# The attention weights of a trunk layer, transposed by DMA in pieces of 1024 keys

## The chip, the core and the metric

The kernel runs on one core of a Trainium2 chip. A core has five engines that work in parallel, each through its own list of instructions in a fixed order: TensorE (PE in the profile, with its weight loads as PEld), VectorE (DVE), ScalarE (ACT), GpSimd (POOL) and SyncE (SP), which here only issues DMA transfers. An instruction that has to wait holds up everything behind it on its engine. The metric is the device time of one execution in microseconds (us), lower is better, and times of several runs are given as their median.

## The reference, cut to what matters

One layer of a hybrid encoder: an RMSNorm and one input projection feed three mixers (a diagonal state-space layer S5, a differential attention, a gated linear recurrence HGRN2). Their outputs are joined, projected, and added to the stream; a gated MLP with a short convolution follows. The sequence has 2048 tokens of width 1024; the attention has 6 heads, the MLP 2816 hidden channels. The change lies in the attention:

```python
def attend(args):
    q_blk, blk = args
    q_pos = blk * Q_BLOCK + jnp.arange(Q_BLOCK)                     # Q_BLOCK = 128
    sc = jnp.einsum('bqhcd,bkhcd->bhcqk', q_blk, k).astype(jnp.float32) * scale
    dist = jnp.abs(q_pos[:, None] - k_pos[None, :]).astype(jnp.float32)
    visible = (k_pos[None, :] // CHUNK) <= (q_pos[:, None] // CHUNK)
    bias = jnp.where(visible[None], -slopes[:, None, None] * dist[None], MASK_VALUE)
    p = jax.nn.softmax(sc + bias[None, :, None], axis=-1)
    w = p[:, :, 0] - lam * p[:, :, 1]
    return jnp.einsum('bhqk,bkhd->bqhd', w, v)
```

Each head has two softmax maps; their difference `w` weighs the values. To multiply `w` by `v`, TensorE needs `w` with the keys on the partitions, but it comes out with the queries there: `w` has to be transposed.

## The kernel before, in words

**The attention.** `phase_attn` (L754) is called twice: a first pass for the query blocks i = 0 to 7, whose rows have L = 128 (i + 1), so up to 1024 keys, and a second pass for i = 8 to 15 with 1152 to 2048 keys. Each pass goes over 6 heads and 8 query blocks, so 48 units of one head and one block. In the second pass there are four score buffers (`t_sc`, two a unit) and two buffers for transposed weights (`t_wt`). A unit is worked in these steps:

- *Scores* (L816): TensorE makes 512 scores at a time (`t_ps`, L832). VectorE adds the bias, writes them to `t_sc`, and keeps a running maximum `t_mx` (L836), each chunk waiting for the one ahead of it. ScalarE takes the exponential of the whole row (L848), once for each of the two maps.
- *Joined* (L854): VectorE forms the difference of the two maps in float32, 1024 keys at a time (L867).
- *Parts* (L881): the float32 weights are split into two float16 parts. For each piece of at most 1024 keys ScalarE casts the high part (L890) and GpSimd subtracts it from the weights, which gives the low part (L891). Both lie in the memory of the second map's scores, the low part LM = 128 · 16 = 2048 elements behind the high part. Behind the loop over pieces SP issues two DMA transposes (L898), one for the high part and one for the low part of the whole row, both from `t_sc` to `t_wt`. A transposed block is 128 x 128.
- *Values* (L904): TensorE multiplies the transposed blocks by the values (`t_po`, L913), in chunks of four blocks: eight products with the high part first, then four with the low part. ScalarE copies the result out (L875, L877).

**What runs beside it.** `weave` (L2084) puts the steps of the attention among those of the other phases: the recurrence (`g_` tiles), the output projection (`o_`), and the MLP (`f_`). The MLP's up and gate projections are the `f_pm` matmuls of L96; its weights are brought through DRAM tiles `Wd` by SP (L143 stores, L148 loads). The down-projection is the `f_pd` matmuls of L1786; in its first half its weights are streamed, `f_dst` loads by SP (L1713), cast to `f_dw`, and its activations come as `f_da` (L1757). The last units of the second pass run beside this half.

**What sets the order.** The program is not run in the order in which it is written. The framework's scheduler fixes a list of instructions for each engine by its own estimate of when each can start. A change to one phase can thus move instructions of all phases on all engines. A transpose on SP waits there until its source is written (by ScalarE, or by GpSimd for the low part); behind it wait the loads and stores of all phases.

Of the kernel before, what the change touches and what calls it, by code (L numbers as in the profile page):

```python
# [753 lines left out]
def phase_attn(K, A, QKd, Vd, Yd, i0, i1, s_bufs, lean):  # L754
# [5 lines left out]
    tc, nc = K.tc, K.nc  # L760
    V = nc.vector
    NT = i1 - i0
    LM = 128 * i1
    base, nlam, lk, gc = A.base, A.nlam, A.lk, A.gc
    with ExitStack() as es:
# [9 lines left out]
        def stack(a, i, parts, h, cols):  # L775
            for r, e in enumerate(parts):
                nc.sync.dma_start(
                    out=a[32 * r:32 * r + 32],
                    in_=QKd[i, e, h * HD:(h + 1) * HD, cols].rearrange("(c r) t -> r c t", c=2),
                )  # L780
# [73 lines left out]
        def joined(h, i, sc):  # L854

            H = heads[h]
            n_ = i - i0
            L = 128 * (i + 1)
            a = mp.tile([128, 2], F32, tag="a", name="t_a")
            V.reciprocal(out=a[:, 0:1], in_=H.la[:, 1, n_:n_ + 1])  # L860
            V.tensor_scalar(
                out=a[:, 1:2], in0=H.la[:, 0, n_:n_ + 1], scalar1=a[:, 0:1], scalar2=nlam[:, 0:1],
                op0=ALU.mult, op1=ALU.mult,
            )
            for k0 in range(0, L, 1024):
                k1 = min(L, k0 + 1024)
                V.scalar_tensor_tensor(  # L867
                    out=sc[0][:, k0:k1], in0=sc[1][:, k0:k1], scalar=a[:, 1:2],
                    in1=sc[0][:, k0:k1], op0=ALU.mult, op1=ALU.add,
                )  # L870
# [10 lines left out]
        def parts(h, i, sc):  # L881

            joined(h, i, sc)
            yield 1
            L = 128 * (i + 1)
            hl = sc[1].bitcast(F16)
            wt = wp.tile([128, 2, i1, 128], F16, tag="w", name="t_wt")
            for k0 in range(0, L, 1024):
                k1 = min(L, k0 + 1024)
                nc.scalar.copy(hl[:, k0:k1], sc[0][:, k0:k1])  # L890
                nc.gpsimd.tensor_tensor(  # L891
                    out=hl[:, LM + k0:LM + k1], in0=sc[0][:, k0:k1], in1=hl[:, k0:k1],
                    op=ALU.subtract,
                )
                if k1 < L:
                    yield 1
            for w in range(2):
                nc.sync.dma_start_transpose(  # L898
                    out=wt[:, w, 0:i + 1, :], in_=hl[:, LM * w:LM * w + L]
                )  # L900
            sc.append(wt)
            yield 1

        def values(h, i, sc):  # L904
# [4 lines left out]
            for c in range(nb):  # L909
# [9 lines left out]
                yield 1  # L919

        stages = ((parts, 3), (values, 4))

        def norm(h):
# [1211 lines left out]
```

## Time and profile before

| | |
|---|---|
| median of 3 runs | 2716.79 us (2714.36 to 2717.66) |
| profiled execution | 2723.9 us |
| its span | 2722.1 us, mean granted TensorE clock 0.934 |
| second pass of the attention (first to last transpose issued) | 811.8 to 1900.0 us |
| transposes | 192: 96 of 1 to 8 blocks, 96 of 9 to 16 |

The profiled execution took 7.1 us more than the median, and its span is 1.8 us shorter than its own time. The profile counts an engine busy while it executes; the rest of the span it waits, and for each wait the trace names what ended it. In a row of the timeline, the numbers are start and duration in us, then engine, line, operation, output and inputs, shapes and count; in brackets is the idle time of the engine ahead of it and who ended it. "SPq" is SP's issue of a DMA; its duration is the time for which SP was taken up by it, and its landing is the end of the transfer.

### The profile page before, as it was taken

The page shows a single profiled execution, that of the slowest core. Times are in us where ns is not written, and L with a number is a line of the kernel's source. Part 1 is how long each engine was busy: PE and PEld are TensorE (multiplying, and loading weights), DVE is VectorE, ACT ScalarE, POOL GpSimd, SP SyncE. Part 2 cuts the span into 40 slices and gives each one's busy share as a digit, 9 for nine tenths or more (in the row PEclk, how much of TensorE's full clock was granted, in tenths as well). Part 3 has the DMA queues.
Part 4 walks back from the last instruction along what each step waited for, and adds up shares of the span by engine and source line. Part 5 has one row for each costly group of instructions (what it writes and reads, how often), then busy time and mean ns, then how long its engine had stood idle before and what let it go on. Part 6 is the DMA issues. An engine that isn't in the chain of part 4 may idle for free.

```text
span 2722.1 us, 42584 instructions
## 1 busy us (share of the span) xinstructions
PE 2408.0 (88%) x15438; PEld 1354.2 (50%) x15438; DVE 1873.5 (69%) x3401; ACT 1316.9 (48%) x2470; POOL 1350.7 (50%) x1149
## 2 busy tenths in 40 slices
PE   5998898888888889769988898598979999999998
PEld 4655556766766764334443444243434444444444
DVE  7467756688869885597788998865455655545565
ACT  6333344667757663564466766633235433333321
POOL 5688612455444542367677677515313344444280
PEclk8899898888989989879999999699989999999999
DMA  7676555467456666655466665688784655554733
GB/s 240 230 214 207 167 161 126 94 133 143 104 125 137 132 135 177 161 122 182 150 182 169 183 173 170 207 276 256 266 312 148 204 168 154 155 148 136 286 99 123
DMA packets 556740, 473.07 MB, mean 174 GB/s; under 512 B 277297, under 2 KB 433265, under 8 KB 555505
## 3 DMA queue, kind: packets, MB, share of 16 engines
q1 hardware_dynamic: 534352, 429.97, 56.0%
q10 hardware_dynamic: 22176, 40.38, 4.0%
q8 instruction: 121, 1.98, 0.3%
q14 instruction: 91, 0.74, 0.1%
HBM read 290.35 MB, written 125.83 MB: 153 GB/s over the span
## 4 chain that ended last, share of the span: by engine, by line
PE 22%; DVE 15%; issue 8%; POOL 7%; ACT 7%; DMA 6%; SPq 1%; ACTq 0%; DVEq 0%; POOLq 0%
PE f_pd L1786 10%; PE f_pm L96 7%; POOL f_k L1863 2%; DVE f_a L61 2%; DMA f_dst<-in_w_down_dram 2%; DVE t_sc L836 2%; DVE f_t L1617 2%; PE o_pm L1493 2%; PE o_pe L1411 2%; DVE t_sc L867 1%; DVE f_w L63 1%; POOL f_u L1863 1%; ACT f_t L1615 1%; ACT f_t L1910 1%; ACT t_sc L848 1%
## 5 line engine op out<-in xcount | busy, mean ns | idle before, releaser
L96 PE MATMUL f_pm<-f_q,f_w 128*128 128x512 f16 x3696 | 836.8, 386 | 30.0 <-DVE f_u L1863 9.2
L96 PEld LDWEIGHTS <-f_w 128*128 128x128 f16 x3696 | 363.3, 99 | 487.5 <-issue 70.1
L1786 PE MATMUL f_pd<-f_dw,f_da 128*128 128x512 f16 x1848 | 407.1, 382 | 2.7 <-DVE f_r L1764 1.5
L891 POOL TENSOR_TENSOR t_sc<-t_sc 128x1024 f16<-128x1024 f32 (+7 forms) x144 | 250.6, 1753 | 302.3 <-ACT t_sc L890 279.1
L1786 PEld LDWEIGHTS <-f_da 128*128 128x128 f16 x1848 | 181.1, 98 | 226.2 <-issue 14.5
L832 PE MATMUL t_ps<-t_k,t_q 96*128 96x512 f16 (+2 forms) x480 | 165.9, 372 | 94.6 <-DVE t_mx L836 80.2
L848 ACT ACTIVATE t_sc<-t_sc,t_nm 128x128 f32<-128x128 f32 (+7 forms) x192 | 230.5, 1201 | 6.6 <-DVE f_a L61 1.1
L836 DVE CUSTOM_DVE_ANT_0 t_sc<-t_ps,t_base,t_mx 128x512 f32<-128x512 f32 (+3 forms) x288 | 185.2, 643 | 18.9 <-PE t_ps L832 10.8
L61 DVE TENSOR_TENSOR f_a<-f_t,f_a 128x512 f16<-128x512 f32 x132 | 154.8, 1192 | 48.3 <-ACT f_a L55 47.8
L913 PEld LDWEIGHTS <-t_wt 128*128 128x128 f16 x2448 | 106.3, 101 | 121.3 <-DMA t_wt<-t_sc 50.4
L867 DVE SCALAR_TENSOR_TENSOR t_sc<-t_sc,t_a 128x1024 f32<-128x1024 f32 (+7 forms) x144 | 164.6, 1169 | 1.6
L96 PE MATMUL g_pq<-g_h,g_w 128*128 128x256 f16 x1152 | 159.2, 299 | 5.1 <-DVE g_sg L1160 2.7
L1863 POOL TENSOR_TENSOR f_t<-f_t,f_t 128x512 f32<-128x512 f32 x66 | 101.6, 1553 | 123.1 <-ACT f_a L55 108.8
L913 PE MATMUL t_po<-t_v,t_wt 128*128 128x64 f16 x2448 | 120.5, 198 | 47.2 <-DMA t_wt<-t_sc 42.4
L96 PE MATMUL g_pv<-g_w,g_h 128*128 128x256 f16 x1152 | 150.3, 288 | 9.2 <-ACT g_w L55 9.2
L1863 POOL TENSOR_TENSOR f_k<-f_k,f_k 128x512 f32<-128x512 f32 x88 | 124.5, 1414 | 51.5 <-ACT f_halo L1907 25.4
L1617 DVE SCALAR_TENSOR_TENSOR f_t<-f_u,f_cw,f_t 128x1024 f32<-128x1024 f32 x88 | 124.1, 1410 | 33.1 <-ACT f_t L1615 32.3
L836 DVE CUSTOM_DVE_ANT_0 t_sc<-t_ps,t_base 128x512 f32<-128x512 f32 (+2 forms) x192 | 120.4, 631 | 34.4 <-PE t_ps L832 13.7
L890 ACT CAST t_sc<-t_sc 128x1024 f16<-128x1024 f32 (+7 forms) x144 | 111.4, 792 | 64.4 <-DVE t_sc L867 63.4
L55 ACT ACTIVATE f_w<-f_sum 128x512 f16<-128x512 f32 x110 | 69.2, 629 | 146.4 <-DVE f_sum L139 62.2
L96 PEld LDWEIGHTS <-g_w 128*128 128x128 f16 x1152 | 121.3, 107 | 36.2 <-issue 6.4
L96 PEld LDWEIGHTS <-g_h 128*128 128x128 f16 x1152 | 116.8, 103 | 36.8 <-issue 10.8
(335 smaller groups left out, 4475.4 us busy)
## 6 DMA issues: line engine op xcount, KB each, us to landing
f_w<-Wd SPq DMA_DIRECT2D x231, 256.0 KB, 3.0
Wd<-f_w SPq DMA_DIRECT2D x154, 256.0 KB, 2.1
Ad<-f_a ACTq DMA_DIRECT2D x154, 256.0 KB, 2.7
f_da<-Ad SPq DMA_DIRECT2D x42, 768.0 KB, 4.9
g_h<-Hd SPq DMA_DIRECT2D x24, 1024.0 KB, 6.7
f_dst<-in_w_down_dram SPq DMA_DIRECT2D x48, 512.0 KB, 4.9
o_wst<-in_w_out_dram SPq DMA_DIRECT2D x24, 512.0 KB, 5.8
f_wst<-in_w_gate_dram SPq DMA_DIRECT2D x22, 512.0 KB, 5.6
```

The costliest lines, as they stand in the source:

```text
L61: nc.vector.tensor_tensor(out=lo, in0=src, in1=hi, op=ALU.subtract)
L96: nc.tensor.matmul(out=out, lhsT=lhs(a, k), rhs=rhs(b, k), start=(n == 0), stop=(n == 3 * nk - 1))
L832: nc.tensor.matmul(out=ps[:, 0:k1 - k0], lhsT=qt[:, c, 128 * (i % 4):128 * (i % 4) + 128], rhs=H.k[:, c, k0:k1], start=True, stop=True,)
L836: V.tensor_tensor_reduce(out=sc[c][:, k0:k1], in0=ps[:, 0:k1 - k0], in1=bs[:, k0:k1], scale=1.0, scalar=-3e38 if j == 0 else mx[:, c, j - ...
L848: nc.scalar.activation(out=sc[c][:, 0:L], in_=sc[c][:, 0:L], func=AF.Exp, scale=SLOPES[h], bias=nm[:, c:c + 1], accum_out=H.la[:, c, n_:n_ ...
L867: V.scalar_tensor_tensor(out=sc[0][:, k0:k1], in0=sc[1][:, k0:k1], scalar=a[:, 1:2], in1=sc[0][:, k0:k1], op0=ALU.mult, op1=ALU.add,)
L890: nc.scalar.copy(hl[:, k0:k1], sc[0][:, k0:k1])
L891: nc.gpsimd.tensor_tensor(out=hl[:, LM + k0:LM + k1], in0=sc[0][:, k0:k1], in1=hl[:, k0:k1], op=ALU.subtract,)
L913: nc.tensor.matmul(out=po, lhsT=wt[:, w, b, :], rhs=vt[:, b, 64 * v:64 * v + 64], start=(b == 0 and w + v == 0), stop=(b == i and w == 1),)
L1617: V.scalar_tensor_tensor(out=t0, in0=u[:, c:n + c], scalar=cw[:, c, m:m + 1], in1=t0, op0=ALU.mult, op1=ALU.add,)
L1786: nc.tensor.matmul(out=ps[t], lhsT=a[:, q, x, tk], rhs=w[:, y, q, :], start=(first and q + x + y == 0), stop=(last and q == n - 1 and y == 1),
L1863: eng.tensor_tensor(out=o, in0=a, in1=b, op=op)
```

## The change: each piece is transposed as soon as it is split

The two transposes move from behind the loop into it. Each piece of at most 1024 keys gets two transposes of its own, one for the high and one for the low part, right behind the two instructions that split it. In the first pass a row is one piece, so it keeps its two transposes and its order. In the second pass a row of L keys is two pieces, of 1024 and of L − 1024 keys: four transposes a unit instead of two, 192 instead of 96, half of them of 8 blocks and half of 1 to 8. The same blocks are moved, and PE, VectorE, ScalarE and GpSimd have the same instructions as before. In the new kernel the transposes are at line 896.

```diff
             for k0 in range(0, L, 1024):
                 k1 = min(L, k0 + 1024)
                 nc.scalar.copy(hl[:, k0:k1], sc[0][:, k0:k1])
                 nc.gpsimd.tensor_tensor(
                     out=hl[:, LM + k0:LM + k1], in0=sc[0][:, k0:k1], in1=hl[:, k0:k1],
                     op=ALU.subtract,
                 )
+                for w in range(2):
+                    nc.sync.dma_start_transpose(
+                        out=wt[:, w, k0 // 128:k1 // 128, :], in_=hl[:, LM * w + k0:LM * w + k1]
+                    )
                 if k1 < L:
                     yield 1
-            for w in range(2):
-                nc.sync.dma_start_transpose(
-                    out=wt[:, w, 0:i + 1, :], in_=hl[:, LM * w:LM * w + L]
-                )
             sc.append(wt)
             yield 1
```

The scheduler makes a new order with it. Three places on SP, in its list of DMA issues (the last group of numbers is the shape; a transpose of 9 blocks is 128x9x128):

At the start of the second pass (query blocks 8 to 9 of head 0), before:

```order
L898 DMA_TRANSPOSE t_wt<-t_sc 128x9x128
L1386 DMA o_wst<-in_w_out_dram 128x2x512
L898 DMA_TRANSPOSE t_wt<-t_sc 128x9x128
L1106 DMA g_h<-Hd 128x16x256
L898 DMA_TRANSPOSE t_wt<-t_sc 128x10x128
L1358 DMA Yd<-g_yo 256x1x512
```

and now:

```order
L896 DMA_TRANSPOSE t_wt<-t_sc 128x8x128
L896 DMA_TRANSPOSE t_wt<-t_sc 128x1x128
L896 DMA_TRANSPOSE t_wt<-t_sc 128x8x128
L896 DMA_TRANSPOSE t_wt<-t_sc 128x1x128
L1386 DMA o_wst<-in_w_out_dram 128x2x512
L1106 DMA g_h<-Hd 128x16x256
L896 DMA_TRANSPOSE t_wt<-t_sc 128x8x128
L896 DMA_TRANSPOSE t_wt<-t_sc 128x2x128
L1358 DMA Yd<-g_yo 256x1x512
```

The four transposes of the first unit now stand together; the loads that stood between and behind its two stand behind all four.

At the start of the streamed half of the down-projection (head 5, query blocks 11 to 13; `f_dst` are the streamed weights), before:

```order
L898 DMA_TRANSPOSE t_wt<-t_sc 128x12x128
L1713 DMA f_dst<-in_w_down_dram 128x2x512
L1713 DMA f_dst<-in_w_down_dram 128x512
L1713 DMA f_dst<-in_w_down_dram 128x2x512
L1713 DMA f_dst<-in_w_down_dram 128x512
L1757 DMA f_da<-Ad_73 128x3072
L1757 DMA f_da<-Ad_73 128x2048
L898 DMA_TRANSPOSE t_wt<-t_sc 128x12x128
L1713 DMA f_dst<-in_w_down_dram 128x2x512
L1713 DMA f_dst<-in_w_down_dram 128x512
L1713 DMA f_dst<-in_w_down_dram 128x2x512 x2
L898 DMA_TRANSPOSE t_wt<-t_sc 128x13x128
```

and now, from the same load of `f_da` on:

```order
L1757 DMA f_da<-Ad_73 128x3072
L1757 DMA f_da<-Ad_73 128x2048
L896 DMA_TRANSPOSE t_wt<-t_sc 128x8x128
L1713 DMA f_dst<-in_w_down_dram 128x2x512
L896 DMA_TRANSPOSE t_wt<-t_sc 128x5x128
L1713 DMA f_dst<-in_w_down_dram 128x512
L896 DMA_TRANSPOSE t_wt<-t_sc 128x8x128
L1713 DMA f_dst<-in_w_down_dram 128x2x512 x2
L896 DMA_TRANSPOSE t_wt<-t_sc 128x5x128
```

All four transposes of query block 11 (12 blocks) now stand ahead of the first `f_dst` loads, where before its last one stood behind four of them. The eight of query blocks 12 and 13 stand one by one among the loads; those of block 13 (14 blocks) stood further on before.

At the last unit, before:

```order
L1713 DMA f_dst<-in_w_down_dram 128x2x512
L1713 DMA f_dst<-in_w_down_dram 128x512 x3
L898 DMA_TRANSPOSE t_wt<-t_sc 128x16x128
L1757 DMA f_da<-Ad_77 128x3072
L898 DMA_TRANSPOSE t_wt<-t_sc 128x16x128
L1757 DMA f_da<-Ad_77 128x2048
```

and now:

```order
L1713 DMA f_dst<-in_w_down_dram 128x2x512
L1713 DMA f_dst<-in_w_down_dram 128x512 x2
L896 DMA_TRANSPOSE t_wt<-t_sc 128x8x128 x2
L1757 DMA f_da<-Ad_77 128x3072
L1713 DMA f_dst<-in_w_down_dram 128x512
L896 DMA_TRANSPOSE t_wt<-t_sc 128x8x128 x2
L1757 DMA f_da<-Ad_77 128x2048
```

One of the four loads of streamed weights now stands behind the first two transposes.

On TensorE the rows are too many to show; counted, they read so. Of the 48 units of the second pass, 22 have fewer matmuls than before between their last score matmul and their first value matmul, 20 have as many, 6 have more. In heads 0 to 2 (24 units) the number falls by 184 in all. For the last unit the list had eight `t_po`, 22 `f_pd`, and the other 40 `t_po`; now nine `f_pd` stand between the two groups. Two units of the second pass move far: the scores of head 3, query block 10, now stand ahead of a stretch of some 500 matmuls of the up-projection, and the last scores of head 5, query block 13, some 270 matmuls sooner. From about 1910 us of the profiled execution before, behind the attention, the lists hold the same work in nearly the same order.

## The prediction

> **What bounds the kernel now.** First the page's totals and the shares of the chain that ended last, then the stretches in which the second pass of the attention runs.
>
> ```profile
> PE 2408.0 (88%) x15438; PEld 1354.2 (50%) x15438; DVE 1873.5 (69%) x3401; ACT 1316.9 (48%) x2470; POOL 1350.7 (50%) x1149
> PE 22%; DVE 15%; issue 8%; POOL 7%; ACT 7%; DMA 6%; SPq 1%; ACTq 0%; DVEq 0%; POOLq 0%
> ```
>
> PE is busy for 88% of the span, so time is won only where it stands idle. By stretch (start:end, length, then busy time and instructions of PE, PEld, DVE, ACT and POOL, granted clock, DMA share, GB/s):
>
> ```profile
> 806.00:1006.00 200.00, 176.69 (x1919) 137.13 (x1918) 175.00 (x426) 132.49 (x242) 95.23 (x77) 0.92 0.59 125
> 1006.00:1240.00 234.00, 182.46 (x1218) 95.94 (x1219) 162.28 (x321) 125.53 (x237) 103.02 (x68) 0.85 0.64 157
> 1706.00:1760.00 54.00, 27.30 (x164) 12.06 (x164) 46.58 (x90) 33.72 (x58) 27.81 (x19) 0.66 0.64 201
> 1760.00:1910.00 150.00, 136.56 (x788) 63.99 (x787) 86.24 (x129) 54.39 (x84) 50.20 (x25) 0.94 0.86 270
> 1910.00:2722.00 812.00, 778.74 (x3596) 353.80 (x3594) 445.76 (x533) 268.03 (x431) 320.31 (x211) 0.98 0.56 182
> ```
>
> The second pass runs from 806 to 1910. PE idles 23 us in the first of these rows, 52 in the second, 27 in the short one before the streamed down-projection, 13 in the next. Behind 1910 nothing of the change is left. Who ends PE's idle time between 806 and 1910 (total us, times, longest), and from 806 to 1240 alone (last row):
>
> ```profile
> PE t_ps L832 <- DVE t_mx L836: 76.3, 54, 7.3
> PE t_po L913 <- DMA t_wt<-t_sc: 28.5, 14, 6.6
> ...
> PE t_po L913 <- DMA t_wt<-t_sc: 20.2, 11, 4.6
> ```
>
> The largest wait, scores behind the running maximum on DVE, isn't touched. The transposed weights are waited for 28.5 us in 14 places. That is the most that the change can take out of PE's idle time directly; 20.2 us of it lies in heads 0 to 2, before 1240.
>
> **What one transpose costs.** The trace has both sizes: the first pass's transposes move 1 to 8 blocks, the sizes of the new ones (first two rows); the second pass's 9 to 16 (last two). Issue time on SP is min/median/max in ns, landing in us.
>
> ```profile
> L898 SPq DMA_TRANSPOSE t_wt<-t_sc x96: 1120/1218/4422, 435.4 to 765.1; - x96
> DMA to landing us min/median/max: 2.2/3.1/7.7
> ...
> L898 SPq DMA_TRANSPOSE t_wt<-t_sc x96: 1244/1538/6122, 811.8 to 1900.0; - x96
> DMA to landing us min/median/max: 3.2/4.2/11.1
> ```
>
> The last transpose of a unit thus lands 4.2 − 3.1 = 1.1 us sooner after its issue. It also no longer follows one that had to wait for the whole row. What is split ahead of it:
>
> ```profile
> L891 POOL TENSOR_TENSOR t_sc<-t_sc 128x1024 f16<-128x1024 f32 x54 | 126.9, 2354 | 196.4 <-ACT t_sc L890 188.3 <-DVE t_mx L836 5.8 <-DVE rs_t L84 2.3
> L890 ACT CAST t_sc<-t_sc 128x1024 f16<-128x1024 f32 x54 | 56.1, 1042 | 44.8 <-DVE t_sc L867 44.5
> ```
>
> A first high piece need not wait for a second cast (up to 1.04 us) nor a first low piece for a second subtraction (up to 2.35). So the first four-block chunk of values can have its high part 1.1 + 1.04 = 2.1 us earlier, its low part 1.1 + 2.35 = 3.5 us. The last chunk gains 1.1 at most. One wait shows it whole (timeline; bracketed, the wait before it):
>
> ```profile
> 1180.35 9.48 SPq L898 DMA_TRANSPOSE t_wt<-t_sc  x2
> 1185.38 2.87 POOL L891 TENSOR_TENSOR t_sc<-t_sc 128x896 f16<-128x896 f32 x1
> 1187.42 0.40 PE L913 MATMUL t_po<-t_v,t_wt 128*128 128x64 f16 x8
> 1192.46 0.45 PE L913 MATMUL t_po<-t_v,t_wt 128*128 128x64 f16 x5 [4.65 <-DMA t_wt<-t_sc]
> ```
>
> PE does the high products of a chunk at 1187.4 and then stands 4.65 us for the low ones, whose transpose couldn't start before POOL's second piece ended at 1188.25. With pieces the low blocks of that chunk have left when POOL turns to the second piece at 1185.38; landing 1.2 + 3.1 us later they are there by 1189.7, and about 2.8 us of the 4.65 go.
>
> **What of it stays.** The order was made anew by the same planner, and it spends the earlier arrival: of the 48 units of this pass 22 have fewer PE matmuls than before between their last score and their first value matmul, 20 as many, 6 more. In heads 0 to 2 the count falls by 7.7 on average (184 over 24 units). At 176.69/1919 = 0.092 us each (row 806:1006) that is 0.7 us in which PE now comes earlier and finds nothing. Per wait the net is between 1.1 − 0.7 = 0.4 and 2.1 − 0.7 = 1.4 us; over the 11 waits between 4.4 and 15.4. Several waits are shorter than that and can give only themselves:
>
> ```profile
> 815.66 0.41 PE L913 MATMUL t_po<-t_v,t_wt 128*128 128x64 f16 x8 [0.42 <-DMA t_wt<-t_sc]
> ```
>
> So I take 7, nearer the lower end. Bounds: 0 (all spent by the order) and 20.2 (every wait gone).
>
> The last unit, whose wait is the longest, gives nothing by my count:
>
> ```profile
> 1887.28 8.92 SPq L1713 DMA_DIRECT2D f_dst<-in_w_down_dram  x4
> 1895.79 4.21 POOL L891 TENSOR_TENSOR t_sc<-t_sc 128x1024 f16<-128x1024 f32 x2
> 1896.24 2.94 SPq L898 DMA_TRANSPOSE t_wt<-t_sc  x1
> 1900.03 4.10 SPq L898 DMA_TRANSPOSE t_wt<-t_sc  x1
> 1900.81 0.61 PE L913 MATMUL t_po<-t_v,t_wt 128*128 128x64 f16 x8 [6.62 <-DMA t_wt<-t_sc]
> 1901.23 6.23 PE L1786 MATMUL f_pd<-f_dw,f_da 128*128 128x512 f16 x22
> 1907.29 1.33 PE L913 MATMUL t_po<-t_v,t_wt 128*128 128x64 f16 x40
> ```
>
> SP was held by loads of the down-projection's weights until 1896.2. Now one of those four stands behind the first two pieces, so the high part lands some 8.92/4 + 1.1 = 3.3 us earlier. But the order leaves only 9 of the 22 f_pd matmuls to cover the low part, which POOL still ends at 1900.0: 13 matmuls at 6.23/22 = 0.28 us are 3.7 us of cover gone. 3.3 won, 3.7 exposed: 0, between −3.3 and +3.7.
>
> **What it adds.** 96 more issues: 192 × 1.22 − 96 × 1.54 = 86 us of SP's time over 1100 us, or 1.8 us a unit. Two early issues (2.4 us) pass while POOL works on the second piece (2.35 us), so the last piece isn't late by itself. Behind them queue the loads and stores of the other phases. SP's own largest wait from 1000 to 1900 is
>
> ```profile
> SPq L143 <- DVE f_w L63: 198.7, 65, 9.5
> ```
>
> for work of DVE, slack that hides most of the 86 us. It doesn't where the weights are streamed:
>
> ```profile
> 1757.15 3.90 SPq L1713 DMA_DIRECT2D f_dst<-in_w_down_dram  x4
> 1762.05 5.60 SPq L898 DMA_TRANSPOSE t_wt<-t_sc  x1
> 1767.76 2.94 SPq L1713 DMA_DIRECT2D f_dst<-in_w_down_dram  x4
> 1770.74 3.42 SPq L898 DMA_TRANSPOSE t_wt<-t_sc  x1
> 1778.19 2.68 SPq L898 DMA_TRANSPOSE t_wt<-t_sc  x1
> ...
> 1764.57 30.02 PE L1786 MATMUL f_pd<-f_dw,f_da 128*128 128x512 f16 x132 [1.07 <-ACT f_dw L55]
> ```
>
> Three transposes behind such loads hold SP 5.60 + 3.42 + 2.68 = 11.7 us, 3.9 each. Now eight stand among them, four of them of a unit that stood further on before: between 8 × 1.2 = 10 and 8 × 3.9 = 31 us, so from −2 to +19.5. The 132 matmuls ran without a wait, so PE has a reserve there. I charge 2.
>
> [...]
>
> **Sum.** −7 + 0 + 2 = −5 us on the profiled run of 2723.9 us (span 2722.1, 1.8 around it): 2718.9. That run lies 7.1 us above the median of 2716.79, and the median moves alike: 2711.8, say 2712.
>
> **Rivals.**
> *The waits really go (faster).* If the order's tightening costs nothing, most of 20.2 and some of the last 8.3 us vanish, and with each long wait its aftermath. A gap of 2.38 us is followed by slower matmuls:
>
> ```profile
> 1870.01 0.58 PE L832 MATMUL t_ps<-t_k,t_q 96*128 96x512 f16 x1 [2.38 <-DVE t_mx L836]
> 1870.39 9.32 PE L1786 MATMUL f_pd<-f_dw,f_da 128*128 128x512 f16 x36
> 1879.76 7.93 PE L1786 MATMUL f_pd<-f_dw,f_da 128*128 128x512 f16 x36
> ```
>
> 36 of them took 9.32 us instead of 7.93, 1.4 us more. 15 us of waits and three such aftermaths make −19: 2698. For it: 20 units keep their places. Against it: 0.7 of 1.1 us spent in heads 0 to 2. [...]
>
> *SP becomes the bound where weights are streamed (slower).* Place: 1757 to 1795, the eight transposes among the f_dst loads. Loads come 19.5 us later at the worst; beyond the reserve PE stands in f_pd, of which nothing else is ready. It decides once the reserve is under 19.5; with 5 us of it (no row measures the reserve) +14.5, less the 7 won earlier: +8, with its aftermaths +10: 2727. For it: 5.60 us for one transpose there and a DMA share of 0.86. Against: SP rests where it waits for freed buffers.
>
> *Nothing moves.* The order takes back all that lands earlier, because the planner packs until PE meets the transposes again: 0 ± 4, 2717.
>
> **Chances.** The forecast has 0.45 (own range 2706 to 2718; the sum's small parts let 0.18 of it fall to faster, 0.26 to no change, 0.01 to slower), the waits really going 0.24, SP as the bound 0.20, nothing 0.11 (0.07 no change, 0.04 slower). One measurement tells about 0.2% (5.4 us) from no change, so: faster (below 2711.4) 0.42, same 0.33, slower (above 2722.2) 0.25. The range reaches to both outer rivals: 2697 to 2730.
>
> **What would show it.** PE's waits for t_wt from 806 to 1910 fall from 28.5 to 15–22 us; if to under 8, the first rival holds; if they stay at 28, the last. Transposes: 192 with a median issue of 1.2 to 1.3 us and landing near 3.1. The 132 f_pd matmuls still take about 30 us; a gap in them <- f_dw means SP as the bound. The wait for t_mx stays within 5 us of 76.3, and PE's busy time behind 1910 is the same. I am wrong if these waits hardly change and the time does: then the new order of the other phases' work, not the transposes, has decided.

## The result: 1.06% slower

| | median, us | range, us |
|---|---|---|
| before | 2717.22 | 2714.36 to 2721.29 (4 runs) |
| changed | 2746.42 | 2745.48 to 2748.39 (4 runs) |

The ratio is 1.0106, 95% interval 1.0092 to 1.0121: 29 us more, where the prediction had 5 us less. The profiled execution of the changed kernel has a span of 2743.6 us.

### The profile page after: what moved, and what is told of

Its sections match the earlier page's. It is cut to its first block, busy times and chain, and to the rows that moved or that the text cites. A ratio compares the mean times of both kernels' runs of the same rounds, so it can differ in the third digit from the quotient of the medians.

```text
span 2743.6 us, 42869 instructions
## 1 busy us (share of the span) xinstructions
PE 2419.0 (88%) x15438; PEld 1359.8 (50%) x15438; DVE 1883.8 (69%) x3401; ACT 1315.7 (48%) x2470; POOL 1351.9 (49%) x1149
```

## The profile after

First the page's totals, then who ended PE's idle time between 800 and 1930 us, and the transposes of that stretch, as they were shown of the kernel before:

```profile
PE 2419.0 (88%) x15438; PEld 1359.8 (50%) x15438; DVE 1883.8 (69%) x3401; ACT 1315.7 (48%) x2470; POOL 1351.9 (49%) x1149
...
PE t_ps L832 <- DVE t_mx L836: 80.0, 53, 7.3
PE t_po L913 <- DMA t_wt<-t_sc: 22.7, 16, 3.6
...
L896 SPq DMA_TRANSPOSE t_wt<-t_sc x192: 1132/1241/5048, 803.0 to 1917.5; - x192
DMA to landing us min/median/max: 2.3/3.2/11.7
```

The change did what it says. The transposes issue in 1.24 us and land in 3.2. PE waits 22.7 us for them where it waited 28.5, 3.6 at the longest where it was 6.6. The wait for `t_mx`, forecast to stay within 5 us of 76.3, is 80.0. The same work of heads 0 to 2, some 2750 matmuls between the first pass and 1110 us of the execution before, takes 345.1 us where it took 330.0:

```profile
771.50:1116.60 345.10, 302.02 (x2755) 212.27 (x2752) 264.80 (x608) 190.20 (x354) 134.27 (x104) 0.89 0.57 132
```

and before, by the same view:

```profile
780.00:1110.00 330.00, 289.52 (x2753) 201.78 (x2751) 257.21 (x608) 191.16 (x355) 130.84 (x104) 0.92 0.62 138
```

PE's idle time grows by 2.6 us (43.1 after 40.5), its busy time by 12.5: the same matmuls, at a mean granted clock of 0.89 after 0.92. Behind the attention little is lost: the last 3599 matmuls take 815.8 us after 812.8, with PE as long busy as before.

```profile
1909.30:2722.10 812.80, 779.44 (x3599) 354.12 (x3597) 445.93 (x534) 268.03 (x431) 320.73 (x211) 0.98 0.56 183
...
1927.80:2743.60 815.80, 779.26 (x3599) 353.83 (x3597) 445.09 (x529) 267.92 (x431) 319.15 (x209) 0.99 0.55 181
```

## The experiments

Two things changed at once: the transposes, and the order that the scheduler made of all phases' work. To part them, the order has to be held while the transposes change, and the other way round. The order is held by dependencies that ask only for order, not for a wait. A kernel that chains all instructions of an engine by them gets the order that it names:

```python
def in_order(tc, nc):
    orders = ...                               # by engine: places in the traced list
    traced = {}
    for i in nc.cur_bb.bb.instructions:
        if "Boundary" not in type(i).__name__:
            traced.setdefault(str(i.engine), []).append(i)
    for short, engine in ENGINES:
        seq = [traced[engine][at] for at in orders[short]]
        for a, b in zip(seq, seq[1:]):
            tc.add_manual_dep(b, a.name, mybir.DependencyInfo(
                mybir.DependencyClass.NoSync, mybir.DependencyReason.DATA), reason="in_order")
```

```diff
     with tile.TileContext(nc, schedule_with_timeline_sim=True) as tc:
         tile_trunk_kernel(tc, *args)
+        in_order(tc, nc)
```

No run holds the kernel before to its own order everywhere and changes nothing else, so the price of these dependencies alone isn't measured. It can't be much: two runs below that carry them, and keep the order of before in most or all places, come out at 1.0011 and 0.9993. All runs below are told as ratios to the kernel before on the same chip; 0.1% is 2.7 us.

### The transposes or the order

First run: the changed kernel's source with the order of the kernel before. On SP:

```diff
-hi (whole row)
+hi, first piece
+hi, second piece
 ...
-lo (whole row)
+lo, first piece
+lo, second piece
```

> The changed kernel's four transposes a unit, but every instruction of PE, VectorE, ScalarE and GpSimd in the order of the kernel before, and on SP too: both high pieces stand where the one high transpose stood, both low pieces where the low one stood. So no piece leaves earlier; 96 more transposes are all that is added. Theory ORDER (the 29 us come from the new order of all phases' work, not from the transposes): within 6 us of the kernel before, 2712 to 2724 us. Theory TRANSPOSES (twice as many of them hold SP and the DMA engines): most of the 29 us are there, 2737 to 2750 us.

Measured: 1.0016 (1.0006 to 1.0026), 4 us slower. Theory ORDER holds.

Second run, the same but for SP:

```diff
-hi (whole row)
+hi, first piece
+lo, first piece
+hi, second piece
 ...
-lo (whole row)
+lo, second piece
```

> As the run ahead of it, with the order of the kernel before on all engines, but the first high, the first low and the second high piece stand where the high transpose stood, and the second low piece where the low one stood: the early departure that the change is about, without its new order. ORDER: the waits for transposed weights shrink as I forecast for the change itself, 5 to 12 us faster than before, 2705 to 2712 us. TRANSPOSES: slower than before by 20 to 30 us, 2737 to 2750 us.

Measured: 1.0065 (1.0050 to 1.0079), 18 us slower. Both theories missed: ORDER had it faster, TRANSPOSES slower by more. What SP waited for from 800 to 1930 us, in the first run and in the second:

```profile
SPq L896 <- POOL t_sc L891: 26.6, 26, 2.8
```

```profile
SPq L896 <- POOL t_sc L891: 67.5, 41, 4.2
```

A first low piece ahead of the second high one makes SP wait for GpSimd, 41 times instead of 26 and for 41 us more, and every load and store behind it waits too. PE's wait for transposed weights did shrink (18.3 us after 22.6). In one place it then stood 4.18 us for `o_re`, whose load had been queued behind such transposes. This lies in the stretch where most is lost: 401 matmuls take 67.5 us there (991.6 to 1059.1 us), and 57.1 in the kernel before (992.0 to 1049.1). That SP's waiting makes the rest of the 18 us too is not shown.

Third run: the source of the kernel before, whole transposes, with the changed kernel's order on every engine.

```diff
-hi, first piece
-lo, first piece
 ...
-hi, second piece
+hi (whole row)
 ...
-lo, second piece
+lo (whole row)
```

> The two whole transposes a unit of the kernel before, but every engine in the order of the changed kernel; on SP the high and the low transpose stand where the second high and the second low piece stand there. ORDER: as slow as the changed kernel or slower, since PE now meets its values with later transposes: 2744 to 2765 us. TRANSPOSES: back to the kernel before, 2714 to 2722 us.

Measured: 1.0142 (1.0122 to 1.0162), 39 us slower. ORDER holds: the new order costs 39 us with the old transposes, and the pieces give 10 of them back (29 remain). PE's waits in this run:

```profile
PE t_po L913 <- DMA t_wt<-t_sc: 42.6, 20, 6.8
```

With pieces it was 22.7 us: 20 us less waiting went with 10 us less time. The 10 us are the difference of two measured ratios, and by their intervals lie between 3 and 17.

### Where the new order costs

The two orders hold the same set of instructions up to certain points on every engine, so one can be followed to such a point and the other from there on. With whole transposes, the new order in one stretch alone (times of the kernel before):

```diff
-order of before, 780 to 1100 us
+order of the change, 780 to 1100 us
```

> Two whole transposes a unit as before; every engine in the changed kernel's order only in the stretch of heads 0 to 2 of the second pass (some 780 to 1100 us), in the order of before everywhere else. The whole new order costs about 38 us. Theory SPREAD (the order is worse everywhere it differs, in proportion to the rows moved: here 1290 of 2841 on PE): 12 to 20 us slower, 2728 to 2736 us. Theory ONE PLACE (the moved unit of head 3 before the up-projection's stretch makes the loss): within 6 us of before.

```diff
-order of before, 1100 to 1450 us
+order of the change, 1100 to 1450 us
```

> As the run ahead of it, with the new order only from some 1100 to 1450 us, where the scores of head 3, query block 10, move ahead of a stretch of some 500 up-projection matmuls. SPREAD: 10 to 15 us slower, 2726 to 2731 us. ONE PLACE: 25 to 38 us slower, 2741 to 2754 us.

```diff
-order of before, from 1450 us on
+order of the change, from 1450 us on
```

> As the two runs ahead of it, with the new order only behind 1450 us (heads 4 and 5, the streamed down-projection, and all behind it). SPREAD: 6 to 10 us slower, 2722 to 2726 us. ONE PLACE: within 6 us of before.

Measured: 1.0083 (1.0063 to 1.0103), 1.0019 (1.0005 to 1.0032) and 1.0011 (0.9996 to 1.0026): 23, 5 and 3 us. ONE PLACE as I had put it falls: the stretch with the moved unit of head 3 costs 5 us. SPREAD isn't right either, for the loss is more than in proportion in heads 0 to 2. The last stretch can't be told from nothing. The three make 31 us of the 39; their intervals are wide enough to hold the rest.

The same from the other side, the changed kernel with the old order in the first of these stretches:

```diff
-order of the change, 780 to 1100 us
+order of before, 780 to 1100 us (a piece stands where its whole transpose stood)
```

> The changed kernel, pieces and new order, but in the stretch of heads 0 to 2 (some 780 to 1100 us) every engine in the order of the kernel before, the pieces on SP where the whole transposes stood. Theory HEADS 0 TO 2 (the new order there makes most of the 29 us, by PE meeting the recurrence's steps on VectorE with nothing in front of them): 15 to 22 us of the 29 go, so 7 to 14 us above before. Rival (the loss is spread over many small places, and taking one stretch back only shifts it): under 8 us go, so above 21 us over before.

Measured: 1.0033 (1.0019 to 1.0047), 9 us over before; 20 of the 29 us went. HEADS 0 TO 2 holds as to the place; its reason is taken up below.

A narrower stretch, around the longest waits and slowest clock of the changed kernel's trace:

```diff
-order of the change, 975 to 1060 us
+order of before, 975 to 1060 us
```

> As the run ahead of it, but the old order only in some 975 to 1060 us, where the trace of the changed kernel shows a wait of 3.74 us for the recurrence (g_ps behind g_s), one of 1.98 us for g_sg, two of 2.2 to 2.5 us, and the clock at 0.55 and 0.50 in two slices of 11.5 us behind them. If the waits and the slow clock behind them make the loss there: 8 to 12 us of the 29 go, 17 to 21 us over before. If not: under 4 us go, 25 us or more over before.

Measured: 1.0050 (1.0033 to 1.0067), 14 us over before; 15 went, more than I expected. Its converse, the kernel before with the new order only there:

> The converse of the run that took the old order back in some 975 to 1060 us: the kernel before with its whole transposes and its order, and the new order only in that stretch. If what is lost there belongs to the order of that stretch alone: 7 to 15 us slower than before. If it hangs on what comes ahead of it (the state in which the new order arrives there): under 4 us.

Measured: 1.0053 (1.0033 to 1.0073), 14 us slower, as expected. The two together (0.50 + 0.53%) make 1.03%, close to the 1.06% of the change. So half of the loss belongs to the order of 85 us of work, with pieces or without.

### Other new orders without pieces

```diff
-LW = [6.0, 0.44, 5.0, 2.5, 0.72, 1.0]
+LW = [6.0, 0.44, 5.0, 2.5, 0.73, 1.0]
```

> The kernel before with one number of the weaving changed by little (the weight of a step of the second pass, 0.72 to 0.73): no instruction, transpose or wait is added, only the planner makes another order, with 5598 of 27302 rows of PE changed. If an order is a draw, whose real time the planner's estimate doesn't hold to 1%, this costs or wins as much as the change does: 10 to 40 us away from before, more likely slower. If it is something particular to the pieces that makes the new order bad: within 8 us of before.

Measured: 1.0073 (1.0058 to 1.0089), 20 us slower, for a change of 0.01 in one weight of the weaving and no other instruction.

```diff
-            for w in range(2):
+            for w in (1, 0):
```

> The kernel before with its two transposes written in the other order, the low part first: no instruction more, but the planner makes another order (3195 of 27302 rows of PE hold another instruction). Theory DRAW (any new order of this stretch costs about what the change's does): 8 to 40 us slower. Rival: within 8 us of before.

Measured: 1.0027 (1.0012 to 1.0041), 7 us slower. That lies just on the rival's side of the line that I drew, so it doesn't decide for DRAW alone; with the run ahead of it and the change itself it is the third new order that the scheduler made of this work, and all three are slower, by 7, 20 and 39 us. Three are few, and none shows how a better order would be found.

### Do the waits give time?

Whole transposes and the old order everywhere, but pieces for seven of the eight units whose weights PE waited for by more than 1 us (the eighth, head 5, query block 9, waited 1.52 us at 1731.7):

```diff
+EARLY = ((0, 8), (0, 14), (1, 14), (2, 11), (2, 12), (2, 14), (5, 15))      # head, query block
 ...
-                for w in range(2):
+                for w in range(2 if L <= 1024 or (h, i) in EARLY else 0):
                     nc.sync.dma_start_transpose(
                         out=wt[:, w, k0 // 128:k1 // 128, :], in_=hl[:, LM * w + k0:LM * w + k1]
                     )
                 if k1 < L:
                     yield 1
+            for w in range(0 if L <= 1024 or (h, i) in EARLY else 2):
+                nc.sync.dma_start_transpose(
+                    out=wt[:, w, 0:i + 1, :], in_=hl[:, LM * w:LM * w + L]
+                )
```

> The order of the kernel before on all engines, whole transposes except for seven units, in which its trace shows PE waiting for transposed weights by more than 1 us; these seven get pieces, the first high, the first low and the second high one where the high transpose stood, the second low one where the low transpose stood. My prediction's step (the waits can be shortened) taken without its price: 4 to 10 us faster than before. The rival, that SP waiting for GpSimd's first low piece delays what stands behind it as much: within 4 us of before, or slower.

Measured: 0.9993 (0.9978 to 1.0007), no difference, though the waits fell by 9 us from 28.5 (in this kernel the line numbers are 1 to 5 higher):

```profile
PE t_po L918 <- DMA t_wt<-t_sc: 19.3, 13, 5.1
```

The outcome is the rival's. Its reason is hardly seen: SP waits 43.3 us for GpSimd's parts, and waited 37.8 before. Two of the seven places, which hold 7 of the 9 us, show another. The wait of 4.65 us that the prediction showed as its example was followed, before, by another one:

```profile
1192.46 0.45 PE L913 MATMUL t_po<-t_v,t_wt 128*128 128x64 f16 x5 [4.65 <-DMA t_wt<-t_sc]
1197.05 7.15 PE L96 MATMUL f_pm<-f_q,f_w 128*128 128x512 f16 x24 [4.14 <-ACT f_part L1578]
```

Now the first is gone, and the second has taken its length:

```profile
1183.20 0.54 PE L918 MATMUL t_po<-t_v,t_wt 128*128 128x64 f16 x13
1192.23 7.88 PE L97 MATMUL f_pm<-f_q,f_w 128*128 128x512 f16 x24 [8.49 <-ACT f_part L1583]
```

4.65 + 4.14 = 8.79 us in two waits have become 8.49 in one. PE was not what the next stage waited for; it was early for it. At 890 us nothing is won either. Before:

```profile
890.79 0.29 PE L913 MATMUL t_po<-t_v,t_wt 128*128 128x64 f16 x4 [2.49 <-DMA t_wt<-t_sc]
...
894.71 1.16 PE L1279 MATMUL g_pb<-g_e 64*128 64x128 f32 x16 [1.87 <-DVE g_e L1272]
...
896.18 2.78 PE L96 MATMUL g_pv<-g_w,g_h 128*128 128x256 f16 x24
```

with pieces for this unit:

```profile
890.65 2.08 PE L1284 MATMUL g_pb<-g_e 64*128 64x128 f32 x16 [3.05 <-DVE g_e L1277]
...
893.35 4.58 PE L97 MATMUL g_pv<-g_w,g_h 128*128 128x256 f16 x24
```

Two short waits of 2.49 and 1.87 us left the matmuls behind them at a granted clock of 1.00 (894.7 to 899.2 us); one of 3.05 us is followed by 16 that take 2.08 instead of 1.16 us and 24 that take 4.58 instead of 2.78. These 2.7 us are more than the 1.3 us by which the waits of these rows shrank. The mean clock of the 30 us around them is 0.83 (870 to 900 us) and was 0.94 before (877 to 907). A little further on a wait of 1.80 us for `t_mx`, which stood there before, is gone. From the value matmuls ahead (876.08 us before, 872.08 with pieces) to the scores behind (902.40 and 899.22), the pieces take 0.8 us more.

## What the order does in the stretch from 975 us

The converse run and the kernel before are the same program but for this stretch, so their rows can be laid side by side. The stretch takes 95.6 us instead of 85.0, some 1 us of it for ten matmuls more in the window:

```profile
974.30:1069.90 95.60, 79.45 (x649) 50.16 (x650) 74.14 (x151) 50.62 (x85) 34.04 (x23) 0.84 0.57 137
```

```profile
975.00:1060.00 85.00, 73.67 (x639) 43.90 (x637) 68.70 (x151) 51.09 (x85) 32.87 (x23) 0.90 0.66 157
```

PE idles 4.8 us more (16.1 after 11.3), and its work takes 5.8 us more at a clock of 0.84 after 0.90. Where it begins, in PE's rows of the kernel before:

```profile
985.79 0.68 PE L1300 MATMUL g_ps<-g_vn,g_kt 64*64 64x64 f32 x16
986.41 0.39 PE L832 MATMUL t_ps<-t_k,t_q 96*128 96x512 f16 x1
988.22 0.38 PE L832 MATMUL t_ps<-t_k,t_q 96*128 96x512 f16 x1 [1.42 <-DVE t_mx L836]
988.83 0.32 PE L832 MATMUL t_ps<-t_k,t_q 96*128 96x384 f16 x1 [0.24 <-DVE t_mx L836]
989.26 0.59 PE L1411 MATMUL o_pe<-o_we,o_ye 128*128 128x512 f16 x1
989.64 0.64 PE L913 MATMUL t_po<-t_v,t_wt 128*128 128x64 f16 x8
990.30 2.29 PE L1411 MATMUL o_pe<-o_we,o_ye 128*128 128x512 f16 x5
992.52 0.68 PE L1300 MATMUL g_ps<-g_vn,g_kt 64*64 64x64 f32 x16
```

and in the new order (the converse run):

```profile
986.23 0.68 PE L1300 MATMUL g_ps<-g_vn,g_kt 64*64 64x64 f32 x16
986.85 0.39 PE L832 MATMUL t_ps<-t_k,t_q 96*128 96x512 f16 x1
987.07 0.25 PE L913 MATMUL t_po<-t_v,t_wt 128*128 128x64 f16 x3
987.16 0.38 PE L832 MATMUL t_ps<-t_k,t_q 96*128 96x512 f16 x1
991.40 0.78 PE L1300 MATMUL g_ps<-g_vn,g_kt 64*64 64x64 f32 x16 [3.86 <-DVE g_s L1283]
...
996.42 0.59 PE L1411 MATMUL o_pe<-o_we,o_ye 128*128 128x512 f16 x1 [1.54 <-DVE g_sg L1160]
```

`g_ps` are two halves of a step of the recurrence; the second half needs `g_s` from VectorE. Before, six matmuls of the output projection (`o_pe`) stood between the halves and filled the time. In the new order they stand behind, and PE waits 3.86 us. VectorE, in the same run, works on an attention piece first:

```profile
985.68 2.97 DVE L867 SCALAR_TENSOR_TENSOR t_sc<-t_sc,t_a 128x1024 f32<-128x1024 f32 x2
988.58 1.10 DVE L1206 TENSOR_TENSOR g_qh<-g_e,g_q 128x512 f32<-128x512 f32 x1
989.60 1.11 DVE L1204 TENSOR_TENSOR g_e<-g_e,g_k 128x512 f32<-128x512 f32 x1
990.63 1.35 DVE L1283 COPY_PREDICATED g_s<-g_mb,g_pb 128x512 f32<-128x512 uint8 x2
```

The waits are no longer than those that the change removed elsewhere, but a slow clock stands behind them. Two slices of 11.5 us of the changed kernel (granted clock: the third number from the end):

```profile
990.00:1001.50 11.50, 9.33 (x81) 6.75 (x82) 8.78 (x20) 4.55 (x10) 4.44 (x3) 0.55 0.69 166
1024.50:1036.00 11.50, 9.61 (x42) 5.03 (x42) 10.98 (x24) 5.42 (x10) 3.51 (x2) 0.50 0.79 172
```

and what answers to them before:

```profile
989.00:1000.50 11.50, 9.91 (x95) 5.44 (x95) 11.50 (x29) 8.01 (x13) 5.38 (x6) 0.80 0.70 167
1022.00:1033.50 11.50, 9.80 (x64) 5.21 (x63) 11.00 (x23) 6.40 (x15) 3.61 (x2) 1.00 0.85 208
```

Behind the wait of 3.86 us the converse run has a clock of 0.58 (990 to 1002 us). A slow clock also stands behind shorter waits: in the kernel before, it is 0.50 from 989.1 to 992.5 us, and the longest wait just ahead is the one of 1.42 us shown above. So these traces show no length of wait at which the clock falls.

The other half of the loss is less well known: 5 to 9 us in heads 0 to 2 outside the stretch from 975 to 1060 us (20 less 15, or 23 less 14), and 5 in head 3. For the first part the traces name a place. The same 550 matmuls, before and in the changed kernel:

```profile
841.10:899.30 58.20, 47.70 (x552) 36.86 (x553) 52.58 (x126) 39.48 (x70) 29.44 (x21) 0.94 0.68 138
...
831.80:897.90 66.10, 57.20 (x550) 44.03 (x551) 54.91 (x126) 40.22 (x72) 31.78 (x22) 0.82 0.63 122
```

They take 66 to 74 us in all four traces with the new order at this place (66.1 in the changed kernel and in the one with the old order from 975 to 1060 us, 71.1 and 74.2 in the two with whole transposes), and 60.3 in the changed kernel with the old order of heads 0 to 2. No run changes this place alone. In the changed kernel PE even idles less here than before (8.9 us after 10.5); what is lost is busy time at a clock of 0.82 after 0.94. And a part of that slow clock has no wait ahead of it:

```profile
843.80:854.10 10.30, 10.30 (x130) 8.39 (x128) 8.40 (x23) 6.58 (x15) 3.50 (x2) 1.00 0.35 67
854.10:860.90 6.80, 6.80 (x44) 4.98 (x43) 4.09 (x9) 1.28 (x2) 0.00 (x0) 0.50 0.13 26
```

PE is busy throughout the first row, as far as the trace tells (it models where matmuls end), and the clock is 0.50 in the second all the same. A second place in this trace has only short waits ahead of it: PE waits 0.70 us before 1005.1 and 0.29 before 1010.8 us, and the clock is 0.50 from 1011.1 to 1017.8. In both, PE had just worked on small float32 matmuls of the recurrence (`g_po`, `g_pl`); no run tests whether that is the reason. So it is shown that the new order costs the time, and that most of what heads 0 to 2 lose is busy time at a slower clock (0.89 after 0.92); that long waits bring the slow clock is read from where they stand, and is not the whole account.

## Why the prediction was wrong

- **What a transpose costs: right.** Issue 1.24 us and landing 3.2 us were forecast as 1.2 to 1.3 and near 3.1.
- **The waits: right in size.** 22.7 us, just above a forecast of 15 to 22; the longest is 3.6 us after 6.6. But the first run, with the pieces at the old places, waits as little (22.6) and is 4 us slower than before, so the size says nothing of the time.
- **The price of 96 more issues: about right.** I charged 2 us; in the old order, with nothing issued sooner, they cost 4 (1.0016). The streamed weights did not suffer: the first 132 matmuls of the down-projection ran as 8 and 124 (3.57 and 27.73 us) with one score matmul between, so the rival "SP becomes the bound where weights are streamed" had the right sign, but its mechanism isn't there. SP as a queue that waits in front of others does cost in the second run, in heads 0 to 2 (the 4.18 us that PE stands for `o_re`). In the changed kernel SP waits no longer for GpSimd's parts than before (33.7 us after 37.8), but 110.7 us for ScalarE's after 57.9; what that costs no run separates.
- **"What of it stays": wrong, the first failed step.** I counted 0.4 to 1.4 us of time for each of 11 waits. The run with pieces at seven units took 9 us out of these waits and nothing that can be told from noise out of the time (0.9978 to 1.0007). A wait at which PE stands is time only if what comes next is ready; at the two places read, `f_part` on ScalarE and `g_e` on VectorE were not.
- **"Sum": wrong, the step that made the sign.** It has no term for the new order of the other phases' work. I had the order at hand, counted PE rows between scores and values in it, and priced it at 0.7 us a unit, for the attention alone. I named the case only in the last sentence, as what would make me wrong, without a chance, and with a sign that did not come: the waits for transposed weights did change, about as forecast. The new order costs 39 us (1.0142), of which the pieces return 10.
- **The aftermath of a wait: seen, but on the wrong side.** I put the slower matmuls behind a long wait into the faster rival only, as time to be won. The new order made more such waits, in heads 0 to 2 five of over 2 us (16.6 us) after three (9.8 us), and 12.5 of the 15.1 us lost there are busy time at a lower clock (0.89 after 0.92). Not all of that clock stands behind a wait.

## What to carry to other kernels

Where a scheduler makes the order from its own estimate, an edit in a woven stretch can bring a new order of everything woven there, and that can cost more than the edit is worth (here 39 us against 10): hold the order, measure the edit alone, then let the scheduler go. Before a wait is counted as time, read what the engine does next and whether that was ready. And look at the granted clock beside the idle time: in heads 0 to 2 PE idled 2.6 us more and was busy for 12.5 us more with the same matmuls.

## What the runs showed that I had not expected

- A change of 0.01 in a weight that only orders work moved the time by 0.73% (1.0058 to 1.0089).
- Half of a loss of 29 us sat in the order of 85 us of work: the new order put into that stretch alone costs 14 us, taking it out again returns 15.
- The clock was 0.50 behind 10.3 us in which PE had been busy without a wait (from 854.1 us in the changed kernel).
- Pieces issued as early as possible on SP are worse than the same pieces issued late (18 us over before against 4). A DMA that waits for its data holds the queue: SP waited 67.5 us for GpSimd instead of 26.6.
